# The last of four modulation groups of the first layer, computed as row sums on VectorE instead of a split-weight product on TensorE

## The chip, the cores and the metric

The kernel runs on one core of a Trainium2 chip. The metric is device time in microseconds (us) of one execution; lower is better. Three runs of the kernel before took 1378.43, 1379.01 and 1379.61 us, so its median is 1379.01 us. One more execution was recorded by the hardware profiler: it took 1379.68 us, and the span from its first to its last instruction is 1377.9 us. All times below that name a moment ("at 44.95") are microseconds from the start of that span.

The engines are TensorE (PE in the profile; its weight loads are PEld), VectorE (DVE), ScalarE (ACT), GpSimd (POOL) and SyncE (SP), whose queue issues most of the DMA transfers. Each engine executes its own instructions in order and waits on semaphores for the others.

## The reference, cut to what matters

The reference is a two-layer network over 256 latent tokens and 256 context tokens, each of width 1024. Every layer first modulates its input: a conditioning vector goes through SiLU and one big product, and the result gives a shift and a scale for every column.

```
def _modulation(cond, w, b):
    m = jax.nn.silu(cond) @ w + b
    return jnp.split(m[:, None, :], 6, axis=-1)

def _modulate(x, shift, scale):
    return x * (1 + scale) + shift
...
        ml = _modulation(c, ada_w[i], ada_b[i])
        mc = _modulation(c_ctx[None, :], ada_w[i], ada_b[i])
        hl = _modulate(x, ml[0], ml[1])
        hc = _modulate(xc, mc[0], mc[1])
...
    x_m = h @ w_up
```

There are two conditioning vectors, `c` for the latents and `c_ctx` for the context. `ada_w[i]` is 1024 x 6144; its first 1024 columns give the shift `ml[0]` of the first half-layer and its second 1024 columns the scale `ml[1]`. In layer 0 the modulated input `h` then goes into the mLSTM mixer, whose first product is `h @ w_up` (1024 x 2048). So nothing of the first big product can be finished before the shift and scale of layer 0 are known for all 1024 columns. That opening is what is changed here.

## The kernel before

**Arithmetic.** Everything is computed to nearly fp32 precision with a rounded high part and a low part: a matrix `x` is split into `h` (a cast to fp32r, on ACT) and `l = x - h` (on DVE), and a product is three matmuls: high by high, high by low, low by high (`mm3`, lines 384 to 386). `split` (lines 389 and 390) does one such pair of casts.

**Layout.** The hidden activations stand transposed: tile `xT[k]` holds columns `128 k` to `128 k + 127` of the input on the 128 partitions, and all 512 tokens along the row. Shift and scale are therefore one number for each partition and conditioning vector. They live in `mod0`, a 128 x 2 x 8 x 2 tile: shift or scale, column tile `k`, conditioning vector `j`.

**Start-up.** `start_up` (line 588) computes shift and scale in four groups of two column tiles, `GROUPS = ((0, 2), (2, 4), (4, 6), (6, 8))`, while the first five output tiles of `w_up` (`m` from 0 to 4, each 128 columns of the product, in five PSUM banks) are accumulated between the groups. The order on PE, DVE and ACT is written by hand in the list `STEPS`, and the order of the loads on the SP queue in the list `LOADS`. A step is a letter and a number:

- `S g`, `ada_split`: splits the four 128 x 1024 tiles of `ada_w` of group `g` (tiles `adaw`) into `adas`: four casts on ACT and four subtractions on DVE (lines 389 and 390).
- `A g`, `ada_rows`: 16 matmuls with the conditioning vectors as the stationary side (line 478) into a 4 x 512 PSUM row, then one copy of it to SBUF on ACT (line 481).
- `T g`, `ada_T`: four PE transposes that turn the row into columns (line 488).
- `M g`, `ada_cols` and `mod_tiles`: two small additions on DVE that write `mod0` (lines 498 and 499); then the modulation of the group's two `xT` tiles (latent half on ACT, line 576; context half on DVE, line 574), and their split into `hT` (lines 389 and 390).
- `W m`: the split of weight tile `m` of `w_up`.
- two digits, `g m`: the part of output tile `m` that group `g` contributes, two column tiles by three matmuls, six matmuls of 128 x 128 by 512 in all.
- `D n`: `n` matmuls on zeros.

The middle of the list reads `M2 13 14 21 S3 20 A3 24 T3 22 23 M3 31 32 33 34 30`. So PE does the parts 13, 14, 21 and 20, the 16 matmuls of `A3`, part 24, the transposes of `T3`, parts 22 and 23, and then the five parts of group 3, which are the first to read `hT[6]` and `hT[7]`. DVE and ACT do `M2`, `S3`, `M3`. 

**Loads.** `LOADS` ends with `... a2 x2 x3 a3`: the weights of group 2 (eight transfers of 256 KB), the `xT` tiles of groups 2 and 3 (two of 256 KB each), the weights of group 3 (eight of 256 KB). A transfer on the SP queue is issued when the one eight places ahead of it has landed. Behind them in the same queue follow the loads of the next stage: tiles `ar` for the background sums and tiles `raw` with the next weights of `w_up`.

**After start-up.** `w_up` (line 699) computes output tiles 5 to 15 with weights that a stream object loads, splits (`_split`, lines 323 and 326) and hands out; `up_evac` (line 681) empties each finished PSUM bank. In the background, `ada_all` and `ada_bg` compute the other five sixths of both layers' modulation in another form, without PE: row `n` of the transposed weights `adaT` (a 128 x 1024 tile `ar`, one output column on each partition) is multiplied by the conditioning vector, broadcast to all partitions (tile `bc`), and summed along the row, in one DVE instruction with an accumulator output (line 516). `ada_all` itself loads the two `bc` tiles (line 549) and puts SiLU on them (line 558, ACT). These sums are spread over the later stages by `tick`.

Of the kernel before, what the change touches and what calls it, by code (L numbers as in the profile page):

```python
# [7 lines left out]
F32 = mybir.dt.float32  # L8
F32R = mybir.dt.float32r
I32 = mybir.dt.int32  # L10
AF = mybir.ActivationFunctionType
ALU = mybir.AluOpType
# [17 lines left out]
CW = 1024  # L30
# [15 lines left out]

NUP = 5
GROUPS = ((0, 2), (2, 4), (4, 6), (6, 8))
LOADS = [(c[0], int(c[1])) for c in "a0 r0 r1 x0 r2 a1 r3 r4 x1 a2 x2 x3 a3".split()]
STEPS = [(c[0], int(c[1])) for c in (  # L50
    "S0 W0 A0 D3 T0 D6 M0 W1 W2 S1 00 01 W3 W4 A1 03 T1 M1 02 04 10 11 S2 A2 12 T2 M2 13 14 21 "
    "S3 20 A3 24 T3 22 23 M3 31 32 33 34 30").split()]

TAIL = {"mout": 4, "aout": 7, "fout1": 6}
WIDE = {"mout": 5, "aout": 7, "fout1": 10}
# [299 lines left out]
class K:  # L355
# [128 lines left out]
    def ada_T(self, g, r):  # L484
# [3 lines left out]
            self.nc.tensor.transpose(pt[:, 4 * i:4 * i + 4], r[0:4, i * 128:(i + 1) * 128], self.ident[0:4, 0:4])  # L488
        return pt

    def ada_cols(self, g, pt):
        nc = self.nc
        f0, f1 = GROUPS[g]
        nf = f1 - f0
        t = self.tiny(8, "adt")[:, 0:4 * nf].rearrange("p (c f b) -> p c f b", c=2, b=2)
        p = pt[:, 0:8 * nf].rearrange("p (c f b) -> p c f b", c=2, b=4)
        b = self.smc("ada_b").rearrange("p (c f) -> p c f", c=2)[:, :, f0:f1].unsqueeze(3).to_broadcast([128, 2, nf, 2])
        nc.vector.tensor_tensor(t, p[:, :, :, 2:4], b, op=ALU.add)
        nc.vector.tensor_tensor(self.mod0[:, :, f0:f1, :], p[:, :, :, 0:2], t, op=ALU.add)
# [42 lines left out]
    def ada_all(self, items):  # L542

        nc = self.nc
        self.bc = []
        for j in range(2):
            r = self.pool.tile([128, 1024], F32, tag="acc", name="bc", bufs=2)
            self.gate(r[0:1, 0:1])
            nc.sync.dma_start(r, self.a["crow"][j:j + 1, :].to_broadcast([128, 1024]))
            self.bc.append(r)  # L550
        self.arq = [(l, c, k) for l, c, k0, k1 in items for k in range(k0, k1)]
        self.art, self.nar = [], 0
        for _ in range(2):
            self.ar_load()
        for _ in range(2):
            yield
        for r in self.bc:
            nc.scalar.activation(r, r, AF.Silu)  # L558
        yield
        for l, c, k0, k1 in items:  # L560
            yield from self.ada_bg(l, c, k0, k1, 2 if l == 0 or c < 2 else 1)
        self.bc = None
# [25 lines left out]
    def start_up(self):  # L588

        nc, st = self.nc, self.st  # L590
        self.hT = []
        self.xcd = self.dr.tile([16, 128, 512], F32, name="xcd")
        self.xmd = self.dr.tile([16, 128, 512], F32, name="xmd")
        self.t2d = {(n, p, j): self.dr.tile([128, 1024], F32, name="t2d")
                    for n, a, b in (("v", 2, 4), ("y", 1, 6)) for p in range(a) for j in range(b)}
        self.xA, self.x1, self.xc, self.xcr = {}, {}, [], []
        w, ps, raws = [], [], []
        src = self.a["ada_w"][0]
        self.adaw, self.xT = {}, []
        for op, g in LOADS:  # L600
            f0, f1 = GROUPS[g] if op != "r" else (0, 0)
            if op == "a":
                wd = 128 * (f1 - f0)
                nk = 512 // wd
                self.adaw[g] = []
                for k in range(8):
                    if k % nk == 0:
                        t = self.uf("adaw")
                        self.adaw[g].append(t)
                    ap = bass.AP(tensor=src.tensor, offset=src.offset + k * 128 * 6 * D + f0 * 128,  # L610
                                 ap=[[6 * D, 128], [D, 2], [1, wd]])
                    c = k % nk * 2 * wd
                    nc.sync.dma_start(t[:, c:c + 2 * wd].rearrange("p (a b) -> p a b", a=2), ap)
            elif op == "x":
                for i in range(f0, f1):
                    x = self.s2("xT")
                    nc.sync.dma_start(x, self.a["tokT"][i])
                    self.xT.append(x)
            else:
                n, _ = st.ids["up", g, 0]  # L620
                r = self.pool.tile([128, 1024], F32, tag="raw" if g < 3 else "ar", name="raw0",
                                   bufs=NRAW if g < 3 else 2)
                nc.sync.dma_start(r, st.ws[n])
                raws.append(r)

        def wsplit(m):
            if m < 3:
                t = self.pool.tile([128, 2, CW], F32R, tag="w", name="w", bufs=NB)
                h, l = t[:, 0], t[:, 1]
            elif m == 3:  # L630
                h, l = [self.pool.tile([128, CW], F32R, tag="acc", name="w0", bufs=2) for _ in range(2)]
            else:
                h, l = [self.pool.tile([128, CW], F32R, tag="u", name="w0", bufs=NU) for _ in range(2)]
            self.split(h, l, raws[m])
            w.append((h, l))
            ps.append(self.ps("up"))

        def part(g, ms):
            for m in ms:
                for k in range(*GROUPS[g]):  # L640
                    c = slice(k * 128, (k + 1) * 128)
                    self.mm3(ps[m], (w[m][0][:, c], w[m][1][:, c]), (self.hT[k][:, 0], self.hT[k][:, 1]),
                             k == 0, k == 7)

        e = mybir.EngineType
        idle = self.ps("idle")
        rows = {}
        with self.tc.manual_schedule(engines={e.PE, e.DVE, e.Activation}):
            for op, g in STEPS:
                if op == "S":  # L650
                    rows[g] = self.ada_split(g)
                elif op == "A":
                    rows[g] = self.ada_rows(g, rows[g])
                elif op == "T":
                    rows[g] = self.ada_T(g, rows[g])
                elif op == "M":
                    self.ada_cols(g, rows.pop(g))
                    self.mod_tiles(range(*GROUPS[g]))
                elif op == "W":
                    wsplit(g)  # L660
                elif op == "D":
                    for _ in range(g):
                        nc.tensor.matmul(idle, self.zero[:, 0:128], self.zero, start=True, stop=True)
                else:
                    part(int(op), [g])
        for m in range(NUP):
            self.up_evac(m, ps[m])
# [1308 lines left out]
```

## Time and profile before

| quantity | value |
|---|---|
| median of three runs | 1379.01 us (1378.43 to 1379.61) |
| the profiled execution, its time | 1379.68 us |
| its span | 1377.9 us |
| DVE busy | 1074.9 us (78%) |
| ACT busy | 719.8 us (52%) |
| moved by DMA | 297.58 MB, mean 216 GB/s |
| background sums, line 516 | 128 of 1217 ns mean |

A page line such as `PE 1349.8 (98%) x6583` gives busy time, share of the span and number of instructions. A timeline row gives the start, the time until the last of the merged instructions ends, the engine, the line, the operation, the tile written and the tiles read, the shape, how many instructions are merged (`x16`), and in square brackets the idle time of the engine just before it and what ended it. A matmul's own duration (0.39 us) is longer than the distance to the next one (about 0.23 us), because matmuls overlap in the array; distances between starts are what counts on PE.

### The profile page before, as it was taken

What the parts mean: (1) busy time and instruction counts of PE and PEld (TensorE: products, weight loads), DVE (VectorE), ACT (ScalarE), POOL (GpSimd) and SP (SyncE); (2) the same over time, 40 slices, a digit from 0 to 9 for tenths busy, and PEclk for the clock granted to TensorE, in tenths of its full rate; (3) what the DMA queues carried; (4) which work ended last, traced back from release to release, by engine and by line L of the source; (5) the groups of instructions that cost most, each with busy time, mean ns of one, the idle gap of its engine ahead of it and who ended that gap; (6) DMA issues with size and microseconds to landing.
All of it is one profiled execution on the core that took longest, in us unless ns stands there. A gap on an engine that the chain in (4) does not pass through costs nothing.

```text
span 1377.9 us, 18614 instructions
## 1 busy us (share of the span) xinstructions
PE 1349.8 (98%) x6583; PEld 1121.5 (81%) x6583; DVE 1074.9 (78%) x1744; ACT 719.8 (52%) x1238; POOL 121.4 (9%) x215
## 2 busy tenths in 40 slices
PE   7999999999999999999999999999999999999997
PEld 3788888888788888878798888888878888888886
DVE  6599757677588696878789977767888889888873
ACT  6585434445544455364644334334557667466660
POOL 0032000011001011120001000000001001000100
PEclk9999999999999999999999999999999999999999
DMA  9689848789666363766747877746887435356760
GB/s 339 232 294 323 284 153 252 236 288 300 215 196 212 108 230 118 255 194 227 234 139 252 291 243 228 220 144 204 304 252 251 150 100 204 111 185 186 253 201 31
DMA packets 97900, 297.58 MB, mean 216 GB/s; under 512 B 12136, under 2 KB 24808, under 8 KB 97808
## 3 DMA queue, kind: packets, MB, share of 16 engines
q1 hardware_dynamic: 68672, 218.52, 48.7%
q0 software_dynamic: 17472, 57.57, 13.2%
q10 hardware_dynamic: 11664, 20.32, 4.1%
q8 instruction: 51, 0.84, 0.3%
q14 instruction: 41, 0.34, 0.1%
HBM read 262.90 MB, written 33.46 MB: 215 GB/s over the span
## 4 chain that ended last, share of the span: by engine, by line
PE 89%; DVE 5%; ACT 2%; DMA 2%; issue 1%; SPq 0%; ACTq 0%; DVEq 0%
PE fin L1318 8%; PE fin L385 6%; PE fin L384 6%; PE fin L386 6%; PE tok L384 6%; PE tok L385 6%; PE tok L386 6%; PE y L385 5%; PE y L386 5%; PE y L384 5%; PE qk L384 4%; PE qk L386 4%; PE qk L385 4%; PE up L384 2%; PE up L386 2%; PE up L385 2%
## 5 line engine op out<-in xcount | busy, mean ns | idle before, releaser
L326 DVE TENSOR_TENSOR w<-raw,w 128x1024 fp32r<-128x1024 f32 (+3 forms) x290 | 348.0, 1202 | 149.0 <-ACT w L323 142.7
L323 ACT CAST w<-raw 128x1024 fp32r<-128x1024 f32 (+3 forms) x290 | 300.3, 1036 | 287.4 <-PE fin L386 78.9
L516 DVE SCALAR_TENSOR_TENSOR junk<-ar,bc 128x1024 f32<-128x1024 f32 x128 | 155.8, 1217 | 4.1 <-ACT bc L558 1.7
L385 PE MATMUL fin<-h,w 128*128 128x512 f32 (+1 forms) x376 | 141.2, 376 | 0.0
L386 PE MATMUL fin<-h,w 128*128 128x512 f32 (+1 forms) x376 | 140.9, 375 | 0.0
L384 PE MATMUL fin<-h,w 128*128 128x512 f32 (+1 forms) x376 | 140.8, 376 | 0.1
L1318 PE MATMUL fin<-h,w 128*128 128x256 f32 (+1 forms) x640 | 112.9, 339 | 0.0
L1318 PEld LDWEIGHTS fin<-h,w 128*128 128x128 f32 x640 | 98.1, 189 | 14.7
L384 PE MATMUL qk<-xc,w 128*128 128x512 f32 x256 | 100.7, 393 | 0.0
L386 PE MATMUL qk<-xc,w 128*128 128x512 f32 x256 | 99.9, 390 | 0.0
L385 PE MATMUL qk<-xc,w 128*128 128x512 f32 x256 | 99.8, 390 | 0.0
L385 PEld LDWEIGHTS fin<-h,w 128*128 128x128 f32 x376 | 70.8, 188 | 13.1 <-DVE h L1210 0.2
L384 PEld LDWEIGHTS fin<-h,w 128*128 128x128 f32 x376 | 70.6, 188 | 13.2 <-ACT h L1209 0.3
L386 PEld LDWEIGHTS fin<-h,w 128*128 128x128 f32 x376 | 70.8, 188 | 12.6
L384 PEld LDWEIGHTS qk<-xc,w 128*128 128x128 f32 x256 | 48.1, 188 | 10.0 <-issue 0.4
L386 PEld LDWEIGHTS qk<-xc,w 128*128 128x128 f32 x256 | 48.1, 188 | 10.0
L385 PEld LDWEIGHTS qk<-xc,w 128*128 128x128 f32 x256 | 48.1, 188 | 9.7
L384 PE MATMUL up<-hT,w 128*128 128x512 f32 x128 | 50.5, 394 | 0.5 <-ACT hT L389 0.5
L385 PE MATMUL up<-hT,w 128*128 128x512 f32 x128 | 50.1, 392 | 0.4 <-DVE hT L390 0.4
L386 PE MATMUL up<-hT,w 128*128 128x512 f32 x128 | 50.1, 391 | 0.3 <-DVE w L390 0.3
L384 PE MATMUL tok<-w,hT 128*128 128x512 f32 x128 | 49.8, 389 | 0.0
L385 PE MATMUL tok<-w,hT 128*128 128x512 f32 x128 | 49.8, 389 | 0.0
(455 smaller groups left out, 3146.4 us busy)
## 6 DMA issues: line engine op xcount, KB each, us to landing
raw<-in_ws SPq DMA_DIRECT2D x287, 512.0 KB, 4.5
ar<-in_adaT SPq DMA_DIRECT2D x80, 512.0 KB, 4.7
adaw<-in_ada_w SPq DMA_DIRECT2D x32, 256.0 KB, 6.7
t2d<-raw ACTq DMA_DIRECT2D x13, 512.0 KB, 6.0
raw<-t2d SPq DMA_DIRECT2D x13, 512.0 KB, 5.7
raw<-in_ws POOLq DMA_DIRECT2D x13, 512.0 KB, 7.8
zr<-fd ACTq DMA_DIRECT2D x33, 128.0 KB, 4.6
xmd<-xr POOLq DMA_DIRECT2D x16, 256.0 KB, 4.6
```

The source lines that it names most:

```text
L323: k.nc.scalar.copy(h[:, :cols], src)
L326: k.nc.vector.tensor_sub(l[:, :cols], src, h[:, :cols])
L384: mm(out, w[0], x[0], start=start, stop=False, skip_group_check=on)
L385: mm(out, w[0], x[1], start=False, stop=False, skip_group_check=on)
L386: mm(out, w[1], x[0], start=False, stop=stop, skip_group_check=on)
L516: nc.vector.scalar_tensor_tensor(o, w, 1.0, self.bc[j], op0=ALU.mult, op1=ALU.mult, accum_out=col[:, k, j:j + 1])
L1318: nc.tensor.matmul(o, a, b, start=k == 0 and i == 0, stop=k == 7 and i == 1)
```

## The change

Group 3 no longer goes through `S3`, `A3` and `T3`. Its four tiles are loaded as transposed weights (rows of `adaT`, step `t3`: shift and scale of column tiles 6 and 7, 512 KB each). The two broadcast conditioning tiles `bc` are now loaded in start-up (step `b0`), between the `xT` tiles of group 2 and those of group 3, and get their SiLU on ACT in a step `B0`. A step `J3` computes the 2 x 2 x 2 columns with eight of the accumulating DVE instructions, one for each tile and conditioning vector, and adds the bias with one more. `ada_all` finds `bc` made and neither loads it nor puts SiLU on it again in its first call. The two halves of split weight tile 3 move from the buffers `acc`, where `bc` now lies, to buffers of kind `u`.

```diff
-LOADS = [(c[0], int(c[1])) for c in "a0 r0 r1 x0 r2 a1 r3 r4 x1 a2 x2 x3 a3".split()]
+LOADS = [(c[0], int(c[1])) for c in "a0 r0 r1 x0 r2 a1 r3 r4 x1 a2 x2 b0 x3 t3".split()]
 STEPS = [(c[0], int(c[1])) for c in (
     "S0 W0 A0 D3 T0 D6 M0 W1 W2 S1 00 01 W3 W4 A1 03 T1 M1 02 04 10 11 S2 A2 12 T2 M2 13 14 21 "
-    "S3 20 A3 24 T3 22 23 M3 31 32 33 34 30").split()]
+    "20 B0 J3 24 22 23 M3 31 32 33 34 30").split()]
...
+    def ada_sums(self, g):
+        nc = self.nc
+        f0, f1 = GROUPS[g]
+        for c, k, w in self.art:
+            for j in range(2):
+                o = self.pool.tile([128, 1024], F32, tag="junk", name="junk", bufs=1)
+                nc.vector.scalar_tensor_tensor(o, w, 1.0, self.bc[j], op0=ALU.mult, op1=ALU.mult,
+                                               accum_out=self.mod0[:, c, k, j:j + 1])
+        m = self.mod0[:, :, f0:f1, :]
+        b = self.smc("ada_b").rearrange("p (c f) -> p c f", c=2)[:, :, f0:f1].unsqueeze(3).to_broadcast([128, 2, f1 - f0, 2])
+        nc.vector.tensor_tensor(m, m, b, op=ALU.add)
...
     def ada_all(self, items):
-        self.bc = []
-        for j in range(2):
+        load = self.bc is None
+        for j in range(2 if load else 0):
+            if j == 0:
+                self.bc = []
...
-        for r in self.bc:
+        for r in self.bc if load else ():
             nc.scalar.activation(r, r, AF.Silu)
...
+            elif op == "t":
+                self.art = []
+                for k in range(f0, f1):
+                    for c in range(2):
+                        t = self.uf("adaw")
+                        nc.sync.dma_start(t, self.a["adaT"][0, c, k])
+                        self.art.append((c, k, t))
+            elif op == "b":
+                self.bc = []
+                for j in range(2):
+                    t = self.pool.tile([128, 1024], F32, tag="acc", name="bc", bufs=2)
+                    nc.sync.dma_start(t, self.a["crow"][j:j + 1, :].to_broadcast([128, 1024]))
+                    self.bc.append(t)
...
-            elif m == 3:
-                h, l = [self.pool.tile([128, CW], F32R, tag="acc", name="w0", bufs=2) for _ in range(2)]
             else:
                 h, l = [self.pool.tile([128, CW], F32R, tag="u", name="w0", bufs=NU) for _ in range(2)]
...
+                elif op == "B":
+                    for t in self.bc:
+                        nc.scalar.activation(t, t, AF.Silu)
+                elif op == "J":
+                    self.ada_sums(g)
                 elif op == "M":
-                    self.ada_cols(g, rows.pop(g))
+                    if g in rows:
+                        self.ada_cols(g, rows.pop(g))
                     self.mod_tiles(range(*GROUPS[g]))
```

On PE the order of all other instructions stays as it was; 16 matmuls and four transposes drop out. The eight sums take the place of `S3`'s subtractions on DVE, and the two SiLU that of its casts on ACT. In `w_up`, DVE, ACT, SP and GpSimd run some of their instructions in a somewhat different order, because the first background step no longer loads; from the end of `w_up` on the orders agree.

## Prediction

> **What bounds the kernel now.** I read the page first, then PE's waits, then the timeline of PE, DVE and ACT around the third and fourth group.
>
> ```profile
> span 1377.9 us, 18614 instructions
> ...
> PE 1349.8 (98%) x6583; PEld 1121.5 (81%) x6583; DVE 1074.9 (78%) x1744; ACT 719.8 (52%) x1238; POOL 121.4 (9%) x215
> ...
> PE 89%; DVE 5%; ACT 2%; DMA 2%; issue 1%; SPq 0%; ACTq 0%; DVEq 0%
> ```
>
> PE is busy for 98% of the span and makes 89% of the chain that ended last. So PE time removed is worth its full length, and PE time lost is lost for good, unless PE would have waited later anyway.
>
> ```profile
> PE adar L478 <- ACT adas L389: 7.0, 1, 7.0
> PE y L385 <- DVE w L326: 2.9, 3, 1.1
> PE zT L1197 <- DVE z L1169: 1.7, 1, 1.7
> ```
>
> These are PE's three longest waits in total (us, times, longest). The first is the opening: PE's first matmul comes at 7.0. The others lie in stages far behind start-up. Nothing between start-up and that stage waits long enough to swallow a shift of some us: a delay of PE in start-up goes to the end.
>
> Now the stretch that changes, PE first, then DVE and ACT.
>
> ```profile
> 44.95 3.86 PE L478 MATMUL adar<-adas,condr 128*4 128x512 f32 x16
> 48.65 0.40 PE L384 MATMUL up<-hT,w 128*128 128x512 f32 x1
> ...
> 49.81 0.39 PE L386 MATMUL up<-hT,w 128*128 128x512 f32 x1
> 50.13 0.41 PE L488 MATMUL adat<-ident,adarow 4*128 4x4 f32 x4
> 50.46 0.50 PE L384 MATMUL up<-hT,w 128*128 128x512 f32 x1
> ...
> 53.35 0.40 PE L384 MATMUL up<-hT,w 128*128 128x512 f32 x1
> 53.59 0.39 PE L385 MATMUL up<-hT,w 128*128 128x512 f32 x1
> ```
>
> ```profile
> 41.50 1.29 DVE L390 TENSOR_TENSOR hT<-xT,hT 128x512 fp32r<-128x512 f32 x2 [0.90 <-ACT hT L389]
> 42.97 4.63 DVE L390 TENSOR_TENSOR adas<-adaw,adas 128x1024 fp32r<-128x1024 f32 x4 [0.18 <-ACT adas L389]
> 50.57 0.17 DVE L498 TENSOR_TENSOR adt<-adat,sm 128x8 f32<-128x8 f32 x1 [2.97 <-PE adat L488]
> 50.77 0.17 DVE L499 TENSOR_TENSOR mod<-adat,adt 128x8 f32<-128x8 f32 x1
> 50.97 0.74 DVE L574 TENSOR_SCALAR xT<-xT,mod 128x256 f32<-128x256 f32 x2
> 52.61 1.30 DVE L390 TENSOR_TENSOR hT<-xT,hT 128x512 fp32r<-128x512 f32 x2 [0.90 <-ACT hT L389]
> ```
>
> ```profile
> 41.89 3.90 ACT L389 CAST adas<-adaw 128x1024 fp32r<-128x1024 f32 x4
> ...
> 51.97 1.12 ACT L389 CAST hT<-xT 128x512 fp32r<-128x512 f32 x2
> ```
>
> PE is never without work here. The part that first reads group 3 starts at 53.35 with the high half of hT[6]; its second matmul, at 53.59, reads the low half. Those halves come just in time: the first of the two casts from 51.97 is done at about 52.6, the first of the two subtractions from 52.61 at about 53.3. Group 3 is thus hidden behind parts 24, 22 and 23 with 0.3 us to spare.
>
> **The change, step by step.**
>
> *PE is relieved.* The 16 matmuls go: 44.95 to 48.65, 3.70 us, or 0.231 each. Without the transposes, part 22 follows part 24 directly: 50.46 - 49.81 = 0.65 becomes 0.23, 0.42 us. Together 4.12 us. Parts 24, 22 and 23 now start at 44.95; they are 18 matmuls, so the last starts at 44.95 + 17 x 0.231 = 48.9 and ends at 49.3. Then PE can only go on with hT[6].
>
> *ACT.* Four casts (3.90 us from 41.89) go, two SiLU come. Such a SiLU is in the trace, with the sum that waits for it:
>
> ```profile
> 65.97 1.06 ACT L558 ACTIVATE bc<-bc 128x1024 f32<-128x1024 f32 x1 [2.06 <-DMA bc<-in_crow]
> ...
> 67.06 1.23 DVE L516 SCALAR_TENSOR_TENSOR junk<-ar,bc 128x1024 f32<-128x1024 f32 x1 [1.67 <-ACT bc L558]
> ```
>
> The sum starts 1.09 us after the SiLU does. In the changed kernel the first SiLU starts at 41.89, so the first sum at 42.98; DVE is free at 41.50 + 1.29 = 42.79. The second SiLU is done a microsecond later, before the second sum needs it. The copy of the row on ACT (line 481) also goes; it is only part of the way to the transposes.
>
> *DVE, the term that decides.* Eight sums replace four subtractions and one of the small additions. All eight write the same scratch tile (`junk`, one buffer), and the instruction order shows from the second on a wait for DVE itself. So each starts only when the one before is completely done. Two consecutive sums of the background, with that wait, show what it costs:
>
> ```profile
> 402.18 1.21 DVE L516 SCALAR_TENSOR_TENSOR junk<-ar,bc 128x1024 f32<-128x1024 f32 x1
> 403.32 0.07 DVE L516 DVE_READ_ACCUMULATOR junk<-ar,bc 128x1 f32 x1
> 403.50 1.23 DVE L516 SCALAR_TENSOR_TENSOR junk<-ar,bc 128x1024 f32<-128x1024 f32 x1
> ...
> 402.49 0.19 ACT L531 COPY mod<-w 1x1 f32<-1x1 f32 x1
> ...
> 782.54 0.08 DVE L516 DVE_READ_ACCUMULATOR junk<-ar,bc 128x1 f32 x1
> 782.66 0.17 DVE L521 SCALAR_TENSOR_TENSOR adav<-adav,sm 128x8 f32<-128x8 f32 x1
> ```
>
> Start to start is 1.32 us (the tiny ACT copy that the second also needs is done at 402.68, long before). Without the wait it would be 1.14, the distance from a sum to its accumulator read, where the next instruction can begin. The accumulator read comes 1.14 us after a sum's start, and an addition that depends on it 0.12 later. So the eighth sum starts at 42.98 + 7 x 1.32 = 52.22, and the bias addition at 52.22 + 1.26 = 53.48. From the second small addition to the modulation it was 50.97 - 50.77 = 0.20 us, so the modulation starts at 53.68 where it was 50.97: 2.71 us later. By the lower bound of 1.14 it is 52.42, 1.45 later. I take 1.32, since the wait is in the changed kernel's order too.
>
> From there the steps are the old ones: hT[6] has its high half at 52.6 + 2.7 = 55.3 and its low half at 53.3 + 2.7 = 56.0. The matmul that reads the low half moves from 53.59 to 56.04. That is 2.45 us later than before, and it carries the whole rest of the kernel with it (lower bound: 1.2).
>
> *What PE's gap does to its clock.* PE now stands still from 49.3 to 55.3, 6.0 us. Behind the opening no single wait of PE was longer than 1.7 us, so the trace shows what such a gap does only at its two ends (the window rows give busy time of PE, PEld, DVE, ACT and POOL, then the granted clock).
>
> ```profile
> 9.51 1.34 PE L478 MATMUL adar<-adas,condr 128*4 128x512 f32 x3
> 11.83 1.32 PE L478 MATMUL adar<-adas,condr 128*4 128x512 f32 x5
> ...
> 1369.88 0.28 PE L386 MATMUL y<-wu,act 128*128 128x256 f32 x1
> ...
> 1372.00:1373.00 1.00, 0.00 (x0) 0.00 (x0) 1.00 (x3) 0.14 (x1) 0.00 (x0) 0.74 0.14 51
> 1373.00:1374.00 1.00, 0.00 (x0) 0.00 (x0) 1.00 (x4) 0.00 (x0) 0.00 (x0) 0.50 0.00 0
> ```
>
> At the end, the last matmul is over at 1370.16, and in the slice from 1372 to 1373 the mean granted clock is 0.74 and then 0.50: it halves some 2.3 us after PE's last work. At the start, three matmuls took the time (1.34 us) in which five went two us later (1.32): a distance of about 0.43 against 0.23 us. The slow state was over before 11.83, at most 4.8 us after the first matmul at 7.0. So a gap of 6.0 us very likely brings the half clock, and PE comes back slow for some 2 to 4 us. The first 0.75 of it is spent waiting for the low half anyway. The rest, 1.25 to 3.25 us, holds 3 to 7.5 matmuls of 0.43, each 0.2 us too long: 0.6 to 1.5 us. I take 1.0; the bounds are 0 (clock kept) and 1.5.
>
> The Trainium skill speaks against the change here: "TensorE: Matmul & The Clock Gate", section "Part 1: The HAM clock gate", states that PE falls to half clock after an idle window of about 3.4 us, with windows that run free of the kernel, and needs about 3.4 us of sustained work to get the full clock back. By that figure alone the cold stretch would cost about 1.7 us (an estimate from that page) and the sum would be 4.15 instead of 3.45. The rows agree in direction; they show the fall after 2.3 us.
>
> *The transfers.* Before, the weights of group 3 were the last eight of start-up.
>
> ```profile
> adaw<-in_ada_w SPq DMA_DIRECT2D x1, 256.0 KB, 7.4
> ...
> 35.00:40.00 5.00, 5.00 (x25) 2.85 (x24) 1.94 (x5) 0.71 (x2) 0.00 (x0) 1.00 1.09 356
> ...
> 50.00:55.00 5.00, 5.00 (x25) 4.04 (x25) 2.37 (x6) 2.19 (x5) 0.00 (x0) 1.00 0.00 0
> ...
> ar<-in_adaT SPq DMA_DIRECT2D x80, 512.0 KB, 4.7
> ...
> bc<-in_crow SPq DMA_DIRECT2D x4, 512.0 KB, 8.7
> ...
> 27.82 1.08 SPq L617 DMA_DIRECT2D xT<-in_tokT  x2
> ```
>
> The issue rows give the count, the size and the median time to landing. The first row is the last weight transfer of group 3, issued at about 34.3, landed at 41.7. The DMA runs full there (356 GB/s). Ahead of the new last tile stand two more transfers of 512 KB (`bc`): 1.05 MB at 356 GB/s is 2.9 us, so it lands at about 44.6, the first of the four some 4 us earlier at 40. They are needed at 42.98, 45.6, 48.3 and 50.9. If the broadcasts move at half that rate, another 2.9 us: 43, 44.5, 46 and 47.5, still just in time. `bc` itself goes out at about 28, where the third `xT` went, and with 8.7 us to land is there at 37, needed at 41.89. So I cost the transfers at 0; the cover is 2 to 5 us. The loads behind them shift by the same 3 to 6 us; the DMA was empty from 50 on, and the first new `w_up` tile is not split before PE frees a buffer, which also comes later. The move of split tile 3 to other buffers and the reordering in `w_up` cost 0: no wait of PE for them stands among its waits.
>
> *Sum.* -4.12 us of PE work, all of which turns into waiting; +2.45 us until group 3 starts; +1.0 us for the clock: 3.45 us longer. The profiled execution (1379.68, 0.67 above the median) would take 1383.1; on the median of 1379.01 that is **1382.4 us**.
>
> **Rivals.**
> *The clock is kept, or returns at once.* Then only 2.45 us are lost: 1381.5. For it: the windows that decide on the clock are not seen, and PE waits for 0.75 us of a cold stretch anyway. Against it: the fall 2.3 us after the last matmul, with a gap of 6.0 here.
> *A transfer comes late.* If the conditioning broadcasts interfere with each other and with the loads in a full queue, so that the last sum waits for its tile or the first for `bc` by 3 us, the sum is 6.5: 1385.5. For it: 8.7 us to land, against 4.7 for a plain tile of that size in its median. Against it: a cover of 2 to 5 us.
> *Faster: PE's 4.12 us come out.* This needs hT[6] at 49.3 instead of 55.3, so the bias addition 6 us earlier, at 47.5, and the sums (47.5 - 1.26 - 42.98) / 7 = 0.47 us apart; the result is 1374.9. The point from which it decides is 0.97 us: with the sums that close, the low half is where it was. Against it: the sums shown take 1.2 us each, and 1.14 is the least distance. What else could give time back is that the background sums start without waiting for `bc` at 67 (1.67 us of DVE); but PE does not wait for DVE there.
>
> **Chances.** The forecast (late group, slow clock) 0.72; clock kept 0.14; late transfer 0.09; faster, by whatever way, 0.05. The measurement of this kernel can tell about 0.2%, 2.8 us, from no change. The forecast and the late transfer lie above it, but the forecast's low end (2.45 + 0.6, with 0.5 us of scatter between runs) touches it, so I give 0.03 of it to no change: slower 0.78, same 0.17, faster 0.05. The range runs from the chain with the clock kept (1381.5, less half a us of scatter) to a loss of 1.5 us at the clock and a late transfer of 2 us (1385): 1381.0 to 1385.0.
>
> **What would show it.** Right: in the changed profile PE idles once, about 6 us ending near 55.3, released by ACT's or DVE's hT; eight sums stand 1.32 us apart from 42.98; the granted clock falls below 1 near 50 to 58, with matmuls 0.43 us apart behind the gap; the rest is the old trace shifted. Wrong: sums 1.14 apart (1.2 us less), a sum released by DMA, no slow matmuls behind the gap, or PE waits in `w_up` that were not there.

## The result, and the profile after

The changed kernel is slower, by more than was forecast and outside the stated range: 1386.07 us in the median of six runs (1384.26 to 1388.38), against 1379.53 before (1378.43 to 1380.94). The ratio is 1.0047, with a 95% interval of 1.0037 to 1.0057, so 5.1 to 7.9 us. Two more sets of runs of the same kernel gave 1.0038 (1.0023 to 1.0054) and 1.0037 (1.0023 to 1.0051); their medians were 4.2 and 4.7 us above those of the kernel before beside them, and both lie inside the stated range. One execution of all that are reported here, 5496.61 us with the warm start and the filled gap, was in a far slower state and is left out of its ratio.

The page of the changed kernel, first its span and engines, then the chain that ended last:

```profile
span 1384.0 us, 18569 instructions
...
PE 1349.8 (98%) x6563; PEld 1122.5 (81%) x6563; DVE 1080.6 (78%) x1755; ACT 715.4 (52%) x1231; POOL 121.1 (9%) x215
...
PE 86%; DMA 5%; DVE 5%; ACT 2%; issue 1%; SPq 0%; ACTq 0%; DVEq 0%
```

PE has 20 matmuls fewer and the same busy time: what it saved came back as slower matmuls, in the opening, behind part 23 and near the end. The chain's larger DMA share lies in the opening too: it now runs back through the loads, up to 41.72 us (the last begins at 33.86 and takes 7.86), while the first sum starts only at 44.35. The timeline of PE around parts 23 and 31:

```profile
40.39 0.41 PE L488 MATMUL adat<-ident,adarow 4*128 4x4 f32 x4
...
50.16 0.39 PE L386 MATMUL up<-hT,w 128*128 128x512 f32 x1
56.41 0.80 PE L384 MATMUL up<-hT,w 128*128 128x512 f32 x1 [5.86 <-ACT hT L389]
57.14 0.80 PE L385 MATMUL up<-hT,w 128*128 128x512 f32 x1
57.73 0.63 PE L386 MATMUL up<-hT,w 128*128 128x512 f32 x1
58.16 0.63 PE L384 MATMUL up<-hT,w 128*128 128x512 f32 x1
...
60.72 0.47 PE L384 MATMUL up<-hT,w 128*128 128x512 f32 x1
61.03 0.39 PE L385 MATMUL up<-hT,w 128*128 128x512 f32 x1
61.25 0.39 PE L386 MATMUL up<-hT,w 128*128 128x512 f32 x1
```

The first row is `T2`, the last transposes that the two kernels share. Behind part 23 PE waits 5.86 us for hT[6]; then matmuls stand 0.43 us apart until about 60.7, and 0.23 apart after that. What hT[6] waited for shows DVE, with ACT's SiLU:

```profile
42.87 1.30 DVE L390 TENSOR_TENSOR hT<-xT,hT 128x512 fp32r<-128x512 f32 x2 [0.90 <-ACT hT L389]
44.35 1.23 DVE L498 SCALAR_TENSOR_TENSOR junk<-adaw,bc 128x1024 f32<-128x1024 f32 x1 [0.18 <-ACT bc L684]
...
45.69 1.23 DVE L498 SCALAR_TENSOR_TENSOR junk<-adaw,bc 128x1024 f32<-128x1024 f32 x1
...
46.95 1.22 DVE L498 SCALAR_TENSOR_TENSOR junk<-adaw,bc 128x1024 f32<-128x1024 f32 x1
...
53.29 1.22 DVE L498 SCALAR_TENSOR_TENSOR junk<-adaw,bc 128x1024 f32<-128x1024 f32 x1
...
54.56 0.17 DVE L502 TENSOR_TENSOR mod<-mod,sm 128x8 f32<-128x8 f32 x1
54.76 0.73 DVE L589 TENSOR_SCALAR xT<-xT,mod 128x256 f32<-128x256 f32 x2
```

```profile
43.26 2.01 ACT L684 ACTIVATE bc<-bc 128x1024 f32<-128x1024 f32 x2
```

The first sum is released by ACT's SiLU, the others follow one another with no wait for a transfer. The second stands 1.34 us behind the first, the next ones 1.27. The granted clock is in the windows (busy time of PE, PEld, DVE, ACT, POOL; then the clock):

```profile
50.00:54.00 4.00, 0.55 (x3) 0.13 (x1) 3.90 (x7) 0.00 (x0) 0.00 (x0) 1.00 0.01 5
54.00:57.00 3.00, 0.59 (x1) 0.29 (x1) 2.03 (x7) 2.12 (x4) 0.00 (x0) 0.51 0.00 0
57.00:61.00 4.00, 4.00 (x10) 3.08 (x10) 0.93 (x3) 1.04 (x1) 0.00 (x0) 0.51 0.00 0
61.00:65.00 4.00, 4.00 (x19) 3.28 (x18) 2.20 (x2) 1.05 (x1) 0.00 (x0) 1.00 0.38 130
...
1187.00:1188.00 1.00, 0.44 (x2) 0.44 (x3) 0.94 (x3) 0.60 (x1) 0.00 (x0) 0.64 0.00 0
1188.00:1190.00 2.00, 2.00 (x12) 1.98 (x10) 0.59 (x2) 1.21 (x3) 0.00 (x0) 0.50 0.00 0
```

Half clock lasts from 54.06 to 60.89, and again for 3.41 us from 1187.28. The second stretch is not in the first profile of the kernel before.

The two spans differ by 6.1 us. I cut them at marks that both have: `T2`; the last matmul ahead of PE's 1.5 us stop near 605 us; the last matmul ahead of its 2.0 us stop near 1180; the end.

| piece | before | after | difference |
|---|---|---|---|
| start to `T2` | 39.02 | 40.39 | 1.37 |
| `T2` to the second matmul of part 31 | 14.57 | 16.75 | 2.18 |
| from there to the stop near 605 | 551.03 | 552.91 | 1.88 |
| to the stop near 1180 | 575.85 | 575.54 | -0.31 |
| to the end | 197.43 | 198.43 | 1.00 |

The marks, first in the kernel before, then in the changed one (the first row of each is the transposes of `T0`; the last of the four matmuls of line 384 starts at 604.62 and at 610.04):

```profile
13.82 0.41 PE L488 MATMUL adat<-ident,adarow 4*128 4x4 f32 x4
...
39.02 0.41 PE L488 MATMUL adat<-ident,adarow 4*128 4x4 f32 x4
...
603.94 1.07 PE L384 MATMUL y<-w,hn 128*128 128x512 f32 x4
606.09 0.50 PE L385 MATMUL y<-w,hn 128*128 128x512 f32 x1 [1.08 <-DVE w L326]
```

```profile
15.21 0.41 PE L488 MATMUL adat<-ident,adarow 4*128 4x4 f32 x4
...
609.36 1.07 PE L384 MATMUL y<-w,hn 128*128 128x512 f32 x4
611.50 0.50 PE L385 MATMUL y<-w,hn 128*128 128x512 f32 x1 [1.07 <-DVE w L326]
```

The second and the third piece hold the sums and what follows straight on them. The difference of the first is already there at `T0` (1.39), ahead of every changed instruction, and the last piece holds the second half-clock stretch. Whether those two belong to the change was the first question.

### The profile page after: what moved, and what is told of

The parts are those of the page before. It is cut to its first block, busy times and chain, and to the rows that moved or that the text cites. A ratio compares the mean times of both kernels' runs of the same rounds, so it can differ in the third digit from the quotient of the medians.

```text
span 1384.0 us, 18569 instructions
## 1 busy us (share of the span) xinstructions
PE 1349.8 (98%) x6563; PEld 1122.5 (81%) x6563; DVE 1080.6 (78%) x1755; ACT 715.4 (52%) x1231; POOL 121.1 (9%) x215
## 4 chain that ended last, share of the span: by engine, by line
PE 86%; DMA 5%; DVE 5%; ACT 2%; issue 1%; SPq 0%; ACTq 0%; DVEq 0%
PE fin L1350 8%; PE fin L384 6%; PE fin L385 6%; PE fin L386 6%; PE tok L384 6%; PE tok L386 6%; PE tok L385 6%; PE y L385 5%; PE y L386 5%; PE y L384 5%; PE qk L384 4%; PE qk L386 4%; PE qk L385 4%; PE up L384 2%; PE up L385 2%; PE up L386 2%
```

## The experiments

**The two kernels again.** No edit.

> The changed kernel once more, unaltered. In the first profile its 6.1 us of longer span fall into four pieces: 1.37 us before the first changed instruction (step T2 at 40.39 instead of 39.02), 2.2 us because hT[6] comes late, 1.84 us because nine matmuls behind PE's gap run at half clock, and about 0.7 us from a second stretch of half clock near 1187. Theory A (the first and the last piece are chance): T2 comes at another time than 40.39 in this profile, and the stretch near 1187 is gone or elsewhere; the gap and its half clock stay. Theory B (all of it belongs to the change): all four pieces come back within 0.3 us. Both: 1384 to 1388 us.

> The kernel before once more, unaltered. Theory A (the opening scatters by itself): T2 starts elsewhere than at 39.02, by as much as 1 us, and the full clock begins at another time than 10.6. Theory B (the opening of the kernel before is fixed): T2 at 39.0 within 0.3 us. Ratio to the kernel before 1.000 either way; a stretch of half clock between 20 and 1370 would show that such stretches do not belong to the change.

The changed kernel had `T2` at 39.76 and half clock from 53.09 to 59.92, and none later up to its last matmul. The kernel before had `T2` at 39.58, the full clock from 12.0, and now itself a half-clock stretch far behind start-up:

```profile
1182.00:1183.00 1.00, 1.00 (x9) 0.94 (x10) 0.31 (x1) 0.73 (x2) 0.00 (x0) 0.89 0.00 0
1183.00:1186.00 3.00, 3.00 (x14) 2.72 (x13) 2.91 (x8) 3.00 (x10) 0.00 (x0) 0.50 0.00 0
1186.00:1187.00 1.00, 1.00 (x9) 1.00 (x9) 1.00 (x4) 0.91 (x3) 0.00 (x0) 0.91 0.00 0
```

So theory A: opening and late stretch come and go in both kernels. The profiles of all runs, those below included, show on what both hang. From `T0` to `T2` all thirteen take 25.13 to 25.21 us, and in the eleven without matmuls on zeros at the start `T2` moves from 39.02 to 41.01 as the full clock comes at 10.56 to 14.59 us, in either kernel (12.01 and 39.58 in this profile of the kernel before, 12.13 and 39.76 in that of the changed one). The late stretch near 1180 came in six of the thirteen. Within a profile the clock changes only at whole multiples of 3.413 us from one another, at steps that lie elsewhere in each profile. The six that lost the clock had 1.44 to 1.72 us of PE work in the emptiest step around PE's stop there, the seven that kept it 1.71 to 2.14. As far as these profiles can tell, it thus hangs on where the steps happen to lie and not on the kernel: two of four profiles of the kernel before and its variants lost the clock there, four of nine of the changed one and its variants.

The kernel before against itself gave 0.9999 (0.9991 to 1.0008). What comes back in the changed kernel is the distance from `T2` to the stop near 605: 569.66 and 569.45, against 565.60 and 565.66.

**PE kept at work in the gap.**

```diff
-    "20 B0 J3 24 22 23 M3 31 32 33 34 30").split()]
+    "20 B0 J3 24 22 23 D9 D9 D4 M3 31 32 33 34 30").split()]
```

> The changed kernel with 22 matmuls on zeros behind part 23, which keep PE at work for 5.0 of the 5.9 us of its gap and delay nothing. Theory A (half clock behind the gap costs 1.8 us beside the late group): the granted clock stays at 1 behind the gap, matmuls of the parts 31 to 30 stand 0.23 us apart, and the time falls by 1.8 us against the changed kernel (0.7 to 2.3 in each execution, as the clock's windows lie), so some 4.5 us above the kernel before. Rival (the half clock costs nothing, since PE would wait for later splits anyway): no change against the changed kernel.

```profile
50.65 5.15 PE L695 MATMUL idle<-zero 128*128 128x512 f32 x22
...
56.62 0.49 PE L384 MATMUL up<-hT,w 128*128 128x512 f32 x1 [0.82 <-ACT hT L389]
57.35 0.50 PE L385 MATMUL up<-hT,w 128*128 128x512 f32 x1 [0.23 <-DVE hT L390]
```

The second matmul of part 31 stands as far behind `T2` as before (57.35 - 40.59 = 16.76), but no slow matmuls follow, and `T2` to the stop is 567.92: 1.5 to 1.7 us less. The ratio falls to 1.0022 (1.0013 to 1.0031), 3.0 us above the kernel before; the time alone, 1.2 us below the changed kernel beside it with overlapping intervals, would not show the gain. Without the half clock, 2.3 us of the stretch remain: the late group.

**Two scratch tiles.**

```diff
+        os = [self.pool.tile([128, 1024], F32, tag="junk", name="junk", bufs=1), self.uf("junk2")]
...
-                o = self.pool.tile([128, 1024], F32, tag="junk", name="junk", bufs=1)
+                o = os[j]
```

> The changed kernel with two scratch tiles for the sums in turn, so that no sum waits for the one just before it. Theory A (each sum waits for the end of the one before, and the chain of sums sets when group 3 starts): sums 1.14 to 1.16 us apart instead of 1.27, the bias addition 0.8 us earlier, the time 0.8 us less than the changed kernel, the gap some 5 us and still followed by half clock. Rival (the sums are limited by reading two fp32 operands and their distance stays 1.27): no change.

```profile
45.25 1.22 DVE L499 SCALAR_TENSOR_TENSOR junk<-adaw,bc 128x1024 f32<-128x1024 f32 x1
...
46.40 1.22 DVE L499 SCALAR_TENSOR_TENSOR junk<-adaw,bc 128x1024 f32<-128x1024 f32 x1
```

Sums now stand 1.15 apart: the shared scratch tile had cost 0.12 us for each. The second matmul of part 31 came 15.84 us behind `T2` (0.91 less), the gap was 4.89 us, and half clock still followed. `T2` to the stop is 568.96, 0.5 and 0.7 less than in the two profiles so far. The time (1.0033, 1.0021 to 1.0046) can't tell so little from the changed kernel.

**A warm start.** Twelve matmuls on zeros ahead of the first group, in the kernel before and, together with those in the gap, in the changed kernel.

```diff
-    "S0 W0 A0 D3
+    "S0 W0 D9 D3 A0 D3
```

> The kernel before with 12 matmuls on zeros ahead of the first 16 matmuls on the conditioning vectors, so that PE works from about 1.5 us on. Theory A (the opening scatters with the free-running windows of the clock: it got the full clock at 10.6 and 12.0 in two profiles, and T2 came at 39.0 and 39.6): full clock before 9, T2 at 38.5 to 39.2, time 0.3 to 1.0 us below the kernel before. Theory B (the opening is set by the first transfers alone): T2 still between 39 and 40.5, no change.

> The changed kernel with both: the 12 matmuls on zeros at the start and the 22 in its gap, so no half clock in start-up at all. Theory A (what is left is the late group alone): T2 as in the kernel before with the same 12, the second matmul of part 31 16.75 us behind T2 instead of 14.57, and a time 2.2 us above that kernel. Theory B (the change also costs about 1 to 1.5 us elsewhere): 3 us or more above it.

Half of this missed. In the kernel before, the full clock came at 4.35, but at 11.18 it was lost again for 3.41 us, as PE had only now and then something to do; `T2` came at 40.99, and the time did not change (1.0002, 0.9993 to 1.0011). So these twelve did not steady the opening. In the changed kernel the clock stayed full from 6.30 to the last matmul, in this one profile. `T2` to the stop was 567.91, 2.3 us above the kernel before, as with the filled gap alone. Its ratio of 1.0025 (1.0015 to 1.0034) is 3.4 us, more than these 2.3, though the interval begins at 2.1; the time does not rule out theory B.

**The moved transfers and SiLU alone.** Against the kernel before; split tile 3 and the first background step are those of the changed kernel too.

```diff
-LOADS = ... a2 x2 x3 a3
+LOADS = ... a2 x2 b0 x3 a3
-    "S3 20 A3 24 T3 22 23 M3 31 32 33 34 30").split()]
+    "S3 B0 20 A3 24 T3 22 23 M3 31 32 33 34 30").split()]
```

> One part of the change alone: the kernel before with the broadcast conditioning tiles loaded in start-up and their SiLU put there (behind the casts of S3), the split tile 3 in the other buffers and the same first background step as in the changed kernel; group 3 still goes through S3, A3, T3. Theory A (the moved transfers, the moved SiLU and the reordering in w_up cost nothing): 0 within 0.5 us of the kernel before. Rival (the broadcasts in the full queue or the reordering carry part of the loss): 1 to 2 us slower, with PE waiting for a split of group 3 or in w_up.

0.9996 (0.9986 to 1.0005), and 565.60 from `T2` to the stop, the same as before to 0.1 us. The broadcasts, their SiLU and the reordering in `w_up` cost nothing that these marks show.

**Half of the sums.**

```diff
-            for j in range(2):
+            for j in range(1):
```

> The changed kernel with four of the eight sums: those for the context's conditioning vector are left out (its columns are zeroed once at the start), so the output is not the reference's. Theory A (the sums' chain sets when group 3 starts): the bias addition comes 4 x 1.27 = 5.1 us earlier, about 9.1 us behind T2, PE's gap shrinks to about 0.8 us, the clock stays full, and the time is 0.5 us above to 3.5 us below the kernel before, 2.9 below if group 3 starts at once: T2 to the second matmul of part 31 is 16.75 - 5.08 = 11.7 instead of 14.57. Rival (a transfer sets it): the gap stays above 3 us.

```profile
49.70 0.17 DVE L503 TENSOR_TENSOR mod<-mod,sm 128x8 f32<-128x8 f32 x1
```

```profile
50.51 0.39 PE L386 MATMUL up<-hT,w 128*128 128x512 f32 x1
51.56 0.50 PE L384 MATMUL up<-hT,w 128*128 128x512 f32 x1 [0.67 <-ACT hT L389]
52.29 0.51 PE L385 MATMUL up<-hT,w 128*128 128x512 f32 x1 [0.23 <-DVE hT L390]
```

`T2` was at 40.67, so the bias addition came 9.03 us behind it, and the second matmul of part 31 11.62. The gap is 0.67 us, the clock stays full, and `T2` to the stop is 562.76, 2.84 below the kernel before, where 2.9 was expected. The time is 0.9990 (0.9981 to 0.9999), 1.7 us less in the medians. With a chain short enough, 2.8 us of PE's saving of some 4.1 come out. The number of sums sets the loss, not a transfer.

**Two sums moved to GpSimd and ACT.** The sums of the first tile as a product on GpSimd and a row sum on ACT, the other six on two scratch tiles, and nine matmuls on zeros behind part 23 (not shown).

```diff
+                if i == 0:
+                    p = self.uf("prod")
+                    nc.gpsimd.tensor_tensor(p, w, self.bc[j], op=ALU.mult)
+                    late.append((p, c, k, j))
+                    continue
...
+        for p, c, k, j in late:
+            nc.scalar.activation(p, p, AF.Identity, accum_out=self.mod0[:, c, k, j:j + 1])
```

> A version meant to beat both: the changed kernel, but the two sums of the first tile are multiplied on GpSimd (which is idle there) and summed along the row on ACT (idle there too), the other six sums stay on DVE with two scratch tiles in turn, and nine matmuls on zeros stand behind part 23. From the profiles: GpSimd takes 1.42 us for 128x512, so 2.84 for each product, 5.7 for both; six sums 1.15 apart end with the bias addition 6 x 1.15 + 0.1 = 7.0 us behind the first, some 4.5 us earlier than in the changed kernel's 54.56 - 44.35 = 10.2 by 3.2. Theory A (only the chain to group 3 and the clock matter): T2 to the second matmul of part 31 is 16.75 - 3.2 = 13.55 instead of the 14.57 of the kernel before, no half clock behind it, and the time is 1.0 us below the kernel before. Rival (DVE slows down while GpSimd works on the same memory, or GpSimd is late): sums more than 1.3 us apart, or the bias addition waits for ACT, and the time is at or above the kernel before.

> The changed kernel a third time, beside the run above. Two medians so far, 1386.1 and 1384.3, against 1379.5 and 1380.1 before. By the profiles the change itself costs 2.2 (late group) and 1.6 to 1.8 (half clock), 4 us in all; the rest is the opening and the late stretch of half clock, which come and go in both kernels. Theory A: 1383 to 1385.5, ratio 1.0025 to 1.0045, and the distance from T2 to the first long PE stop behind 600 us is 569.5 again, 3.9 above the 565.6 of the kernel before. Theory B (the change costs 6 us): ratio above 1.0045.

The mixed version is the slowest of all: 1.0056 (1.0041 to 1.0070). DVE and GpSimd shut each other out:

```profile
44.75 3.41 DVE L504 SCALAR_TENSOR_TENSOR junk<-adaw,bc 128x1024 f32<-128x1024 f32 x1
...
48.09 3.41 DVE L504 SCALAR_TENSOR_TENSOR junk<-adaw,bc 128x1024 f32<-128x1024 f32 x1
...
51.44 1.22 DVE L504 SCALAR_TENSOR_TENSOR junk<-adaw,bc 128x1024 f32<-128x1024 f32 x1
```

```profile
43.65 6.78 POOL L501 TENSOR_TENSOR prod<-adaw,bc 128x1024 f32<-128x1024 f32 x2 [42.58 <-ACT bc L693]
```

Two sums took 3.41 us instead of 1.22, just while GpSimd worked; with GpSimd done, they are back at 1.22. The bias addition came 15.4 us behind `T2` (55.05 - 39.63), later than in the changed kernel. Half clock came too, from 56.50 to 63.33, in spite of the nine matmuls, and `T2` to the stop is 571.80. The rival was right, and more strongly than it said. The changed kernel beside it, for the third time: `T2` at 41.01, 570.08 from there to the stop, half clock from 55.55 to 62.38 and once more for 3.41 us from 697.26.

**One tile each way.** The last group is cut in two: column tile 6 goes through S, A and T, tile 7 through four sums, three of them ahead of and one behind the small additions of tile 6.

```diff
-GROUPS = ((0, 2), (2, 4), (4, 6), (6, 8))
+GROUPS = ((0, 2), (2, 4), (4, 6), (6, 7), (7, 8))
-LOADS = ... a2 x2 b0 x3 t3
+LOADS = ... a2 x2 a3 b0 x3 x4 t4
-    "20 B0 J3 24 22 23 M3 31 32 33 34 30").split()]
+    "S3 B0 20 A3 J4 24 T3 22 23 P3 K4 H3 M4 31 32 33 34 30 41 42 43 44 40").split()]
```

(`J4` makes three sums, `P3` the additions and the modulation of tile 6, `K4` the fourth sum, `H3` the split of tile 6.)

> A second version meant to beat both, without GpSimd: of the last two column tiles the first goes through S, A and T as in the kernel before (half as many splits, 16 matmuls of half the width), only the second is made by sums (four, on two scratch tiles), three before and one behind the small additions of the first; and the five parts of w_up of the first tile run before those of the second. From the rows: PE saves half of 3.70, 1.85 us; DVE needs 2 x 1.16 + 4 x 1.15 = 6.9 us behind hT[5] and has hT[6] ready at about 51.5 and hT[7] at about 53.4 on the time scale of the first profile of the kernel before, while PE comes to the first at 51.4 and to the second at 54.8. Theory A (the late chain is what spoiled the change, and with the chain short enough PE's saving comes out): no gap of PE above 0.5 us in start-up, T2 to the first long stop behind 600 us 565.6 - 1.8 = 563.8, time 1.8 us below the kernel before. Rival (narrow transfers of 512 bytes a row make the weights of the first tile late, or hT[6] is late by more than PE saves): PE waits 1.5 us or more at part 31, no gain.

```profile
46.26 1.22 DVE L498 SCALAR_TENSOR_TENSOR junk<-adaw,bc 128x1024 f32<-128x1024 f32 x1
...
49.69 0.16 DVE L513 TENSOR_TENSOR adt<-adat,sm 128x4 f32<-128x4 f32 x1
...
50.41 1.22 DVE L498 SCALAR_TENSOR_TENSOR junk<-adaw,bc 128x1024 f32<-128x1024 f32 x1
...
51.75 0.69 DVE L390 TENSOR_TENSOR hT<-xT,hT 128x512 fp32r<-128x512 f32 x1
...
53.50 0.69 DVE L390 TENSOR_TENSOR hT<-xT,hT 128x512 fp32r<-128x512 f32 x1 [0.74 <-ACT hT L389]
```

PE has no gap between `T2` and the parts of tile 7, `T2` to the stop is 563.61 (563.8 was expected), and the time is 1377.35 us: 0.9982 (0.9973 to 0.9991) of the kernel before, 2.5 us faster. This version beats both kernels.

## Why the prediction was wrong

*PE's saving: right.* Part 23's last matmul started 9.77 us behind `T2` (50.16 - 40.39), by the prediction 48.9 - 39.02 = 9.9. All of the saving turned into waiting.

*The sums: right, a little too long.* The bias addition came 14.17 us behind `T2`, predicted 14.46. Only the second sum stood 1.34 behind the first; the others stood 1.27 apart, not 1.32. The pairs of the background, from which I took 1.32, wait for ACT as well, so the extra 0.05 may be theirs. The late group cost 2.18 (2.3 with the gap filled) where 2.45 stood. That the sums' number sets it is shown by the half of them.

*The half clock: the mechanism was right, the size was not.* This is the term that was mis-sized: 1.0 us with an upper bound of 1.5. In the first profile the nine matmuls from 57.14 to 61.03 took 3.89 us, where nine at 0.228 take 2.05: 1.84 lost. Against the filled gap, which has the same late group, the three profiles of the changed kernel give 1.74, 1.53 and 2.16 (569.66, 569.45 and 570.08 less 567.92). I had read the length of the slow stretch off the opening, 2 to 4 us behind PE's return. It was 4.48 (56.41 to 60.89) in the first profile and 4.1 and 5.3 in the two others, since its end is not counted from PE's return. Between the opening and the last matmul the slow stretches of all profiles last 3.41 us or twice that, and in the first profile the second one begins 332 x 3.413 us behind the first (1187.28 - 54.06 = 1133.22): the clock is decided at fixed steps. The step in which PE came back had 1.06 us of work (56.41 to 57.47) and did not bring the clock back, and neither did 0.72 and 1.93 us in the two other profiles or 3.00 us in the mixed version. So the whole next step was slow too. How much work a step needs is not settled: in the opening of the first profile a step with 2.75 us of it (9.68 to 13.10) brought the full clock. The free-running windows that the Trainium skill names in "TensorE: Matmul & The Clock Gate", "Part 1: The HAM clock gate", agree with these steps. The Trainium skill's 3.4 us of slow work would have given a sum of 4.15 (the estimate of the prediction), which is nearer to the 4.1 that the profiles show.

*The transfers: right.* No sum waited for one, and the broadcasts alone cost nothing.

*The range: too narrow by what lies outside the sum.* The late group and the half clock make 4.1 us in the mean of the three profiles (569.73 - 565.60), which is 1383.1 on the old median, inside the range. What lies outside the sum is more than the half microsecond that I allowed for it. The median of three from which I counted was low by half a microsecond (1379.01, against 1379.53 of the six). The opening moves `T2` by up to 2 us (39.02 to 41.01), and the first profile of the kernel before had the earliest. A late stretch of half clock (0.76 us of the first pair: its 1.00 in the last piece less the 0.24 named below) comes in some executions of either kernel. The medians of the two later sets, 1384.29 and 1384.79, would have been inside the range: that the first one lay outside is in part chance.

What stays open: the three timings put the loss at 4.2 to 6.5 us in their medians, the marks at 4.1. Another 0.24 us comes with the change behind the last matmul, whose end lies 7.71 to 7.75 us ahead of the span's end in the five profiles of kernels with step `S3` and 7.96 to 7.99 in the eight without it; why, no run shows. The rest has either sign in other runs: the filled gap's loss is larger by the time than by the marks (3.0 and 2.3), the gain of one tile each way too (2.65 in the medians, and 2.0), that of the half of the sums smaller (1.7 and 2.8). Chance in the opening and in the late stretches is of that size, but that it is the whole of the rest was not shown.

*The rivals.* The clock was not kept in any profile of the unaltered changed kernel. No transfer was late. A gain, as the faster rival had it, needed sums less than 0.97 us apart or fewer of them: with four of the eight it came.

## What to carry to other kernels

When work moves from the busiest engine to another one, write down when its result is needed and when the other engine, in its order, can have it; the saving counts only up to that point, and of the splits tried here half and half was the best. A gap of 4.9 to 5.9 us in TensorE's work cost here its own length and then a slow stretch behind it, which ended only with a whole step of 3.41 us of work; one of 0.67 us left the clock alone. Filling the gap saves the slow stretch, not the gap itself. An effect of a few us in 1380 is better read as a distance between two marks in the trace than from whole times: from `T2` to the stop the kernel before repeated within 0.1 us and the changed one within 0.6, while six whole times of the kernel before scattered by 2.5.

## What the hardware did that I had not expected

GpSimd and VectorE shut each other out when both read two fp32 tiles from SBUF: sums of 1.22 us took 3.41, while GpSimd needed 3.39 for each product (6.78 / 2). The Trainium skill says so, in "SBUF — State Buffer", section "Who interferes with whom": a VectorE instruction with two SBUF inputs contends with a GpSimd instruction that reads SBUF, and the loser is blocked for the whole instruction. The trace agrees: in each 3.4 us one sum and one product came out, in step.

Ending the wait of a sum for its predecessor by a second scratch tile saved 0.12 us each, 1.27 to 1.15. And once the clock is full, occasional work does not hold it: with the twelve matmuls on zeros it was lost at 11.18, in the middle of the first group's matmuls, and near 1180 a single stop of 1.7 us lost it in six profiles of thirteen.
